# Two pairs of experts summed in PSUM, scattered in one visit among the gate products

## The chip, the core and the metric

The kernel runs on one core of one Trainium2 chip. The metric is the device time of one execution in microseconds: 1461.55 us, the median of three runs (1460.7 to 1462.7). The engines of a core are TensorE (PE in the profile; its weight loads are a row of their own, PEld), VectorE (DVE), ScalarE (ACT), GpSimd (POOL) and SyncE (SP), which issues the transfers between HBM and the on-chip memory SBUF. TensorE writes its results to PSUM.

## The reference, cut to what matters

The program is two model blocks, one behind the other. The last part of the second, a mixture of 32 experts over 512 tokens of width 1024, is what the change touches. Each token takes two experts of one group:

```python
def routed_experts(ht, expert_idx, combine_w, w_gate, w_up, w_down):
    ...
    def expert_block(args):
        xb, e = args
        g = xb @ w_gate[e]
        u = xb @ w_up[e]
        return (jax.nn.silu(g) * u) @ w_down[e]
    ys = lax.map(expert_block, (xs, block_expert)).reshape(n_rows, d)
    contrib = (ys[dest].astype(jnp.float32) * w_sorted[:, None]).astype(ht.dtype)
    return jnp.zeros((t, d), ht.dtype).at[tok_sorted].add(contrib)
...
x = x + hierarchical_moe(h, ...)      # then a final RMS norm, which is the output
```

Each expert has three float32 matrices of 2 MB (gate and up 1024 x 512, down 512 x 1024), 192 MB for all 32.

## The kernel before

**Pairs of experts.** Each expert has room for 64 tokens; two experts make a pair of 128 rows, 16 pairs in all (`NP`), and two pairs make a block of four experts. `gather(b)` (L1330) collects the tokens of a block, transposed, into the tile `xT`, as products of the token rows (split in two parts, `xh` and `xl`) with 0/1 matrices. `up_products(pr, "g")` and `up_products(pr, "u")` (L1515) are the gate and up products of a pair: eight steps `k`, two experts side by side in 64 columns each, accumulated in the PSUM tiles `pga` and `pgb`. `silu` (L1530) and `combine` (L1535) make the hidden rows `hh`; `hidden` (L1559) transposes them on TensorE; `down` (L1587) makes the products with the down weights in `pgy` and `pgz`, and `weigh` (L1576) scales each row by its token's weight and splits the result in two parts, `yh` and `yl`.

**Selection and scatter.** `select_t(pr)` (L1541) transposes the pair's 0/1 matrix on TensorE into `selT` and makes the rows' weights `wcol` by small products. `scatter(pr)` (L1603) adds a pair's results to the token rows `xtok`: eight steps (four groups of 128 tokens, two halves of 512 columns), each with two matmuls of 128x512 into a PSUM tile `pgs` (`yh`, then `yl`; two such tiles alternate, and the gather uses them too) and one add on VectorE (L1611).

**Order.** TensorE runs the loop of L1695 in the order in which it is written (`tc.manual_schedule`); other engines and queues are ordered by a scheduler. For each pair `pr` the order is: gate products of `pr`, down products of `pr - 1`, up products of `pr`. `hidden(pr - 1)` stands among the gate products of an odd pair (after `k` = 3) and ahead of those of an even pair. The scatter of `pr - 1` is a generator that is advanced from inside the up products: two steps after `k` = 1, 3, 5 and 7 (L1716), and after `k` = 7 the selection of the next pair. These four interruptions are called visits below. After an odd pair the gather of the next block follows.

**Weights.** The experts' weights come in loads of 1 MB, four for each matrix kind of a pair, through a ring of 15 tiles (`ring`, some of them allocated late) and five tiles that are used once (`pre`). `load` (L1203) issues the next loads on SP in the order of their use; each waits until TensorE has done with the tile's previous content. Preceding stages load their weights through the same queue in pieces (`wraw`) that ScalarE and GpSimd split.

Of the kernel before, what the change touches and what calls it, by code (L numbers as in the profile page):

```python
# [11 lines left out]
F32R = mybir.dt.float32r  # L12
# [16 lines left out]
NE = 32  # L29
# [95 lines left out]
def body(ctx, tc, a, out, stop=None, dbg=None):  # L125
# [86 lines left out]
    with ExitStack() as c1:  # L212
# [10 lines left out]
        def ptt():  # L223
            return pt_.tile([128, 1024], F32, name="pt")
# [1270 lines left out]
    SC = {}  # L1495
# [45 lines left out]
    def select_t(pr):  # L1541

        b, q = pr // 2, 2 * (pr % 2)
        p = ptt(BF16)
        sb = [SELB[b][:, i, q:q + 2].rearrange("p e s -> p (e s)") for i in range(4)]
        for i in range(4):
            nc.tensor.transpose(p[:, 128 * i:128 * i + 128], sb[i], identb)
        t = (SC["wk2"] if pr % 2 else wk_).tile([128, 512], F32R, name="selT")
        ACT(t, p, AF.Copy)
        pw = ptt()  # L1550
        for i in range(4):
            mm(pw[:, :9], sb[i], aux[:, i, pr], start=i == 0, stop=i == 3)
        w = wk_.tile([128, 2], F32, name="wcol", bufs=4)
        for z in range(2):
            V.tensor_reduce(w[64 * z:64 * z + 64, 0:1], pw[64 * z:64 * z + 64, 3 * z:3 * z + 3], axis=AX.X, op=OP.add)
        V.tensor_reduce(w[:, 1:2], pw[:, 6:9], axis=AX.X, op=OP.add)
        SC[pr] = [t, w]
# [17 lines left out]

    def weigh(ps, w, c, n=512, rows=128):  # L1576

        yh, yl = [SC["wk2"].tile([128, 512], F32R, name=f"{t}{c // 512}")[:rows, :n] for t in ("yh", "yl")]
        p = ps[c // 512][:rows, c % 512:c % 512 + n]
        ACT(yh, p, AF.Identity, scale=w[:rows, 0:1])  # L1580
        V.scalar_tensor_tensor(yl, p, w[:rows, 0:1], yh.bitcast(F32), op0=OP.mult, op1=OP.subtract)  # L1581
        return c, n, yh, yl
# [17 lines left out]
                G.tensor_tensor(xv, hv, lv, op=OP.add)  # L1600
        SC[pr] += [weigh(ps, SC[pr][1], c) for c in (0, 512)]

    def scatter(pr):  # L1603

        for i in range(4):
            for c, n, *ys in SC[pr][2:]:
                p = pg.tile([128, 512], F32, name="pgs", bufs=2)[:, :n]
                for q, y in enumerate(ys):
                    mm(p, SC[pr][0][:, 128 * i:128 * i + 128], y, start=q == 0, stop=q == 1)  # L1609
                x = SC["xtok"][:, i, c:c + n]  # L1610
                V.tensor_tensor(x, x, p, op=OP.add)  # L1611
                yield
        del SC[pr][2:]

    def free(n):

# [3 lines left out]
    def overflow(n_ov):  # L1620
        with tc.For_i(0, n_ov, 1) as bi:  # L1621
            e = nc.sync.value_load(ids[:1, bass.ds(bi, 1)], min_val=0, max_val=NE - 1)
            wv = {}
            for nm, src, kk in (("g", eg, 8), ("u", eu, 8), ("d", ed, 4)):
                for hf in range(2):
                    v = free(len(wv)).rearrange("p (k f) -> p k f", k=kk // 2)
                    nc.sync.dma_start(v, src[bass.ds(e, 1)].rearrange("o (p k) f -> p (o k) f", k=kk)[:, kk // 2 * hf:kk // 2 * (hf + 1)])
                    wv[nm, hf] = v
            ws = free(7)
            sc = [ws[:, 256 * c:256 * c + 256].rearrange("p (i s) -> p i s", i=4) for c in range(2)]  # L1630
            for c in range(2):
                V.tensor_tensor(sc[c], i64[:, None, :].to_broadcast([128, 4, 64]),
                                ov[:, c, :, None].to_broadcast([128, 4, 64]), op=OP.is_equal)
            s_ = free(6)[:, :1024].bitcast(F32R).rearrange("p (i e s) -> p i e s", i=4, e=4)
            V.memset(s_.bitcast(F32), 0.0)
            V.tensor_tensor(s_[:, :, 0], sc[0], sc[1], op=OP.add)
            V.tensor_scalar(ov, ov, float(-CAP), None, op0=OP.add)
            SEL["o"] = s_
            run(gather("o"))
            x = XT.pop("o")  # L1640
            ps = [pg.tile([128, 512], F32, name=n) for n in ("pga", "pgb")]
            for p, nm in zip(ps, "gu"):
                for k in range(KT):
                    mm(p[:64], x[:, k, :64], wv[nm, k // 4][:, k % 4], start=k == 0, stop=k == KT - 1)
            w = wk_.tile([128, 2], F32, name="wcol", bufs=4)
            pw = ptt()
            for c in range(2):
                for i in range(4):
                    mm(pw[:64, :1], sc[c][:, i], cw[:, c, i:i + 1], start=c == 0 and i == 0, stop=c == 1 and i == 3)
            for i in range(4):  # L1650
                mm(pw[:64, 1:2], s_[:, i, 0].bitcast(F32), r4[:, i:i + 1], start=i == 0, stop=i == 3)
            V.tensor_copy(w[:64], pw[:64, :2])
            sg = ws[:, 512:1024]
            ACT(sg[:64], ps[0][:64], AF.Silu, scale=w[:64, 1:2])
            h = ws[:, 1024:1536]
            V.scalar_tensor_tensor(h[:64].rearrange("p (k f) -> p k f", k=4),
                                   ps[1][:64].rearrange("p (f k) -> p k f", k=4), w[:64, 1:2],
                                   sg[:64].rearrange("p (f k) -> p k f", k=4), op0=OP.mult, op1=OP.mult)
            p = ptt()
            for k in range(4):  # L1660
                nc.tensor.transpose(p[:, 64 * k:64 * k + 64], h[:64, 128 * k:128 * k + 128], ident[:64, :64])
            hT_ = SC["wk2"].tile([128, 512], F32, name="hh").rearrange("p (k s) -> p k s", k=4)
            ACT(hT_[:, :, :64], p[:, :256].rearrange("p (k s) -> p k s", k=4), AF.Copy)
            pT = ptt()
            for i in range(4):
                nc.tensor.transpose(pT[:64, 128 * i:128 * i + 128], s_[:, i, 0].bitcast(F32), ident)
            t = wk_.tile([128, 512], F32R, name="selT")
            ACT(t[:64], pT[:64], AF.Copy)
            ps = [pg.tile([128, 512], F32, name=n) for n in ("pga", "pgb")]
            SC["o"] = [t[:64], w]  # L1670
            for c in range(2):
                for k in range(4):
                    mm(ps[c][:64], hT_[:, k, :64], wv["d", k // 2][:, k % 2, 512 * c:512 * c + 512], start=k == 0, stop=k == 3)
                SC["o"].append(weigh(ps, w, 512 * c, 512, 64))
            run(scatter("o"))
# [1 line left out]
    NP = NE // 2  # L1677
    n_ov = None

    def steps_of(g, n):  # L1680
        def go():
            for _ in range(n):
                next(g, None)
        return go

    with tc.manual_schedule(engines={mybir.EngineType.PE}):

        g0 = gather(0)
        for _ in range(2):
            next(g0)  # L1690
        pga = up_products(0, "g", {3: [lambda: run(g0)], 7: [lambda: select_t(0)]})
        s_ = silu(0, pga)
        h = combine(0, up_products(0, "u"), s_)
        hT_ = None
        for pr in range(1, NP):  # L1695
            b = pr // 2

            turn = []
            if pr % 2:
                pga = up_products(pr, "g", {3: [lambda: turn.append(hidden(pr - 1, h))]})  # L1700
                hT_ = turn[0]
            else:
                hT_ = hidden(pr - 1, h)
                pga = up_products(pr, "g")
            down(pr - 1, hT_)
            if pr == 1:
                select_t(1)
            s_ = silu(pr, pga)
            if pr % 2 and b + 1 < NE // 4:
                select(b + 1)  # L1710
            if pr == 4:
                n_ov = nc.values_load(ids[:1, 16:17], min_val=0, max_val=16)
            sc_ = scatter(pr - 1)
            two = steps_of(sc_, 2)
            if pr < NP - 1:
                after = {1: [two], 3: [two], 5: [two], 7: [steps_of(sc_, 9), lambda: select_t(pr + 1)]}  # L1716
            else:
                after = {2: [two], 5: [two]}
            h = combine(pr, up_products(pr, "u", after), s_)
            run(sc_)  # L1720
            if pr == NP - 2:

                fnw = wk_.tile([128, D], F32, name="sel")
                for c in range(2):
                    p = ptt()
                    for k in range(4):
                        col = C("final_norm_w_2")[:, 4 * c + k:4 * c + k + 1]
                        nc.tensor.transpose(p[:, 128 * k:128 * k + 128], col.to_broadcast([128, 128]), ident)
                    ACT(fnw[:, 512 * c:512 * c + 512], p, AF.Copy, scale=ROOT)
            if pr % 2 and b + 1 < NE // 4:  # L1730
                run(gather(b + 1))


    xtok = SC["xtok"]
# [99 lines left out]
```

## Time and profile before

| | |
|---|---|
| median of three runs | 1461.55 us |
| profiled execution: its time, its span | 1461.99 us, 1460.1 us |
| granted TensorE clock, mean | 0.984 |
| busy: PE, DVE, ACT, POOL | 1385.2, 724.1, 558.0, 443.2 us |
| expert weights, loads of 1 MB or parts of one | 60 gate, 61 up, 60 down, 5 `pre`, 12 parts |
| bytes moved | 279.35 MB |

The page cuts the span in 40 equal slices and gives for each the busy tenths of every engine. The experts begin in slice 26 or so, near 950 us. Matmul ends are modelled, so the places to read are the starts: the pace of weight loads tells how fast TensorE really goes. [...]

### The profile page before, as it was taken

The numbers are of one execution on the slowest core, as the hardware profiler recorded it, in microseconds if no ns is written. First come the engines' busy times: TensorE is split into PE (matmuls) and PEld (weight loads), VectorE is DVE, ScalarE is ACT, GpSimd is POOL, SyncE is SP. The second block draws the span as 40 slices with busy tenths as digits, with TensorE's granted clock in tenths as the row PEclk, the third lists the DMA queues.
The fourth block names the chain that finished last, engine by engine and source line by source line (L and its number), as shares of the span: only waits on it lengthen the run. The fifth ranks groups of instructions, "written<-read, shape, count | busy, mean of one in ns | idle before, by whom it ended". The sixth has DMA issues, their size and how long they took to land. (4 is left out here: it accounts for less than half of the span.)

```text
span 1460.1 us, 21828 instructions
## 1 busy us (share of the span) xinstructions
PE 1385.2 (95%) x8468; PEld 1028.3 (70%) x8468; DVE 724.1 (50%) x1360; ACT 558.0 (38%) x1055; POOL 443.2 (30%) x364
## 2 busy tenths in 40 slices
PE   6999999999999999989989999799999999999996
PEld 5998999999899987767867788644345343543432
DVE  5656775454777537768654353423333233332224
ACT  5355554434554552768654343321111111111112
POOL 3432215643222687372676324411000000000002
PEclk9999999999999999989999999899999999999998
DMA  6322113332211343223452117778999999999981
GB/s 200 94 70 53 40 44 103 95 94 55 57 48 49 88 123 89 70 73 101 122 156 63 58 58 255 304 286 318 420 404 420 404 405 419 408 419 408 395 325 59
DMA packets 158266, 279.35 MB, mean 191 GB/s; under 512 B 15568, under 2 KB 125392, under 8 KB 134096
## 3 DMA queue, kind: packets, MB, share of 16 engines
q1 hardware_dynamic: 158160, 277.92, 52.1%
q8 instruction: 68, 1.11, 0.3%
q14 instruction: 38, 0.31, 0.1%
HBM read 275.79 MB, written 2.10 MB: 190 GB/s over the span
## 5 line engine op out<-in xcount | busy, mean ns | idle before, releaser
L174 POOL TENSOR_TENSOR wl<-wraw,wh 128x512 fp32r<-128x512 f32 (+1 forms) x248 | 328.3, 1333 | 456.3 <-ACT wh L173 428.5
L173 ACT ACTIVATE wh<-wraw 128x512 fp32r<-128x512 f32 (+1 forms) x248 | 150.2, 616 | 217.3 <-PE pp L181 49.4
L180 PE MATMUL pp<-slab,wh 128*128 128x264 f32 (+1 forms) x536 | 155.1, 290 | 8.2 <-ACT wh L173 7.3
L181 PE MATMUL pp<-slab,wh 128*128 128x264 f32 (+1 forms) x536 | 155.7, 291 | 2.9 <-DVE slab L201 2.6
L182 PE MATMUL pp<-slab,wl 128*128 128x264 f32 (+1 forms) x536 | 154.8, 289 | 1.0 <-POOL wl L174 1.0
L1755 POOL TENSOR_TENSOR xtok<-xtok,sel 128x512 f32<-128x512 f32 x4 | 5.0, 1272 | 455.1 <-ACT xT L1749 455.1
L182 PE MATMUL pm<-slab,wl 128*128 128x512 f32 (+1 forms) x320 | 122.3, 383 | 5.6 <-POOL wl L174 5.5
L181 PE MATMUL pm<-slab,wh 128*128 128x512 f32 (+1 forms) x320 | 121.0, 379 | 3.4 <-DVE slab L194 3.4
L180 PE MATMUL pm<-slab,wh 128*128 128x512 f32 (+1 forms) x320 | 122.0, 383 | 1.0 <-ACT slab L193 1.0
L1522 PE MATMUL pgb<-ring,xT 128*64 128x512 f32 x504 | 122.4, 601 | 0.0
L180 PE MATMUL p<-slab,wh 128*128 128x264 f32 (+1 forms) x400 | 115.7, 289 | 3.3 <-DVE rs L244 1.6
L1611 DVE TENSOR_TENSOR xtok<-xtok,pgs 128x512 f32<-128x512 f32 x128 | 82.4, 682 | 65.5 <-PE pgs L1609 65.5
L182 PE MATMUL p<-slab,wl 128*128 128x264 f32 (+1 forms) x400 | 113.1, 283 | 0.0
L181 PE MATMUL p<-slab,wh 128*128 128x264 f32 (+1 forms) x400 | 112.8, 282 | 0.0
L180 PEld LDWEIGHTS pp<-slab,wh 128*128 128x128 f32 x536 | 103.6, 194 | 8.6 <-ACT wh L173 7.3
L1522 PE MATMUL pga<-ring,xT 128*64 128x512 f32 x480 | 108.1, 597 | 0.0
L1581 DVE SCALAR_TENSOR_TENSOR yl<-pgy,wcol,yh 128x512 fp32r<-128x512 f32 x16 | 12.0, 750 | 192.2 <-ACT yh L1580 192.2
L181 PEld LDWEIGHTS pp<-slab,wh 128*128 128x128 f32 x536 | 103.5, 193 | 4.5 <-DVE slab L201 3.9
L182 PEld LDWEIGHTS pp<-slab,wl 128*128 128x128 f32 x536 | 103.7, 194 | 1.5 <-POOL wl L174 1.5
L180 PEld LDWEIGHTS p<-slab,wh 128*128 128x128 f32 x400 | 75.5, 189 | 5.1 <-issue 1.7
L1522 PEld LDWEIGHTS pgb<-ring,xT 128*64 128x64 f32 x504 | 32.6, 136 | 62.9 <-issue 61.1
L181 PEld LDWEIGHTS p<-slab,wh 128*128 128x128 f32 x400 | 75.5, 189 | 0.0
(419 smaller groups left out, 3102.0 us busy)
## 6 DMA issues: line engine op xcount, KB each, us to landing
ring<-in_expert_up_w_dram SPq DMA_DIRECT2D x61, 1024.0 KB, 11.5
ring<-in_expert_gate_w_dram SPq DMA_DIRECT2D x60, 1024.0 KB, 11.7
ring<-in_expert_down_w_dram SPq DMA_DIRECT2D x60, 1024.0 KB, 9.6
wraw<-in_w_in_dram SPq DMA_DIRECT2D x108, 256.0 KB, 2.9
wraw<-in_w_out_dram SPq DMA_DIRECT2D x48, 256.0 KB, 2.9
wraw<-in_xk_w_dram SPq DMA_DIRECT2D x16, 256.0 KB, 3.0
wraw<-in_xv_w_dram SPq DMA_DIRECT2D x16, 256.0 KB, 2.7
wraw<-in_xq_w_dram SPq DMA_DIRECT2D x16, 256.0 KB, 3.0
```

Of the source, the lines that this page charges most:

```text
L173: ACT(h, raw, AF.Copy)
L174: G.tensor_tensor(lo, raw, h.bitcast(F32), op=OP.subtract)
L180: mm(ps, lh, rh, start=first, stop=False)
L181: mm(ps, lh, rl, start=False, stop=False)
L182: mm(ps, ll, rh, start=False, stop=last)
L1522: mm(p[64 * z:64 * z + 64], XT[b][:, k, 64 * (q + z):64 * (q + z) + 64], W(src, 2 * pr + z, k), start=k == 0, stop=k == KT - 1)
L1581: V.scalar_tensor_tensor(yl, p, w[:rows, 0:1], yh.bitcast(F32), op0=OP.mult, op1=OP.subtract)
L1611: V.tensor_tensor(x, x, p, op=OP.add)
L1755: G.tensor_tensor(x, x, fnw[:, :512], op=OP.mult)
```

## The change

The scatter takes one or more pairs. With two, the four matmuls of a step (two for each pair) accumulate in one `pgs` tile, and there is one add for both pairs. The scatter leaves the up products: pairs `pr - 3` and `pr - 2` are scattered in one visit among the gate products of an odd pair `pr` (after `k` = 3), between the two halves of the pair's selection, which is now a generator too, and ahead of `hidden(pr - 1)`. For an even pair the gather stands between the two halves of the selection. Pair 14 is scattered alone behind the last up products. The tiles `selT`, `yh` and `yl` get more buffers (4, 2 and 2), since results now wait longer, and the kernel asks for 1024 bytes of dynamic DMA scratch, where it had left the size to its default.

```diff
-        t = (SC["wk2"] if pr % 2 else wk_).tile([128, 512], F32R, name="selT")
+        t = wk_.tile([128, 512], F32R, name="selT", bufs=4)
         ACT(t, p, AF.Copy)
+        yield
         pw = ptt()
...
-        yh, yl = [SC["wk2"].tile([128, 512], F32R, name=f"{t}{c // 512}")[:rows, :n] for t in ("yh", "yl")]
+        yh, yl = [SC["wk2"].tile([128, 512], F32R, name=f"{t}{c // 512}", bufs=2)[:rows, :n] for t in ("yh", "yl")]
...
-    def scatter(pr):
+    def scatter(*prs):
 
         for i in range(4):
-            for c, n, *ys in SC[pr][2:]:
+            for parts in zip(*[SC[pr][2:] for pr in prs]):
+                c, n = parts[0][:2]
                 p = pg.tile([128, 512], F32, name="pgs", bufs=2)[:, :n]
-                for q, y in enumerate(ys):
-                    mm(p, SC[pr][0][:, 128 * i:128 * i + 128], y, start=q == 0, stop=q == 1)
+                ys = [(SC[pr][0], y) for pr, part in zip(prs, parts) for y in part[2:]]
+                for q, (t, y) in enumerate(ys):
+                    mm(p, t[:, 128 * i:128 * i + 128], y, start=q == 0, stop=q == len(ys) - 1)
                 x = SC["xtok"][:, i, c:c + n]
                 V.tensor_tensor(x, x, p, op=OP.add)
                 yield
...
             if pr % 2:
-                pga = up_products(pr, "g", {3: [lambda: turn.append(hidden(pr - 1, h))]})
-                hT_ = turn[0]
+                def middle():
+                    st = select_t(pr)
+                    next(st)
+                    if pr > 2:
+                        run(scatter(pr - 3, pr - 2))
+                    run(st)
+                    return hidden(pr - 1, h)
+
+                got = []
+                pga = up_products(pr, "g", {3: [lambda: got.append(middle())]})
+                hT_ = got[0]
             else:
+                st = select_t(pr)
+                next(st)
+                run(gather(b))
+                run(st)
                 hT_ = hidden(pr - 1, h)
                 pga = up_products(pr, "g")
...
-            sc_ = scatter(pr - 1)
-            two = steps_of(sc_, 2)
-            if pr < NP - 1:
-                after = {1: [two], 3: [two], 5: [two], 7: [steps_of(sc_, 9), lambda: select_t(pr + 1)]}
-            else:
-                after = {2: [two], 5: [two]}
-            h = combine(pr, up_products(pr, "u", after), s_)
-            run(sc_)
+            h = combine(pr, up_products(pr, "u"), s_)
...
-            if pr % 2 and b + 1 < NE // 4:
-                run(gather(b + 1))
+        run(scatter(NP - 2))
...
-    nc = _bacc.Bacc("TRN2", target_bir_lowering=False, num_devices=1)
+    nc = _bacc.Bacc("TRN2", target_bir_lowering=False, num_devices=1, dynamic_dma_scratch_size=1024)
```

On TensorE, one visit of the scatter among the up products of an odd pair before the change; the number behind a name tells its buffers apart, `ring11` and `ring12` hold the two experts' weights:

```order
L1522 MATMUL pgb_11868<-ring11_11617,xT_11723 64x512
L1522 MATMUL pgb_11868<-ring12_11627,xT_11723 64x512
L1609 MATMUL pgs_11873<-yh0_11858,selT_11560 128x512
L1609 MATMUL pgs_11873<-yl0_11859,selT_11560 128x512
L1609 MATMUL pgs_11877<-yh1_11862,selT_11560 128x512
L1609 MATMUL pgs_11877<-yl1_11863,selT_11560 128x512
L1522 MATMUL pgb_11868<-ring11_11617,xT_11723 64x512
```

Two steps of one pair, two matmuls each, stood between up products; now the 16 up product matmuls of a pair stand in one run, and this is gone.

On TensorE, the beginning of the visit among an odd pair's gate products in the changed kernel, from the last transpose of the selection on:

```order
L1547 MATMUL pt3_11844<-identb_10552,selb_11614 128x128
L1612 MATMUL pgs_11851<-yh0_11599,selT_11280 128x512
L1612 MATMUL pgs_11851<-yl0_11600,selT_11280 128x512
L1612 MATMUL pgs_11851<-yh0_11794,selT_11495 128x512
L1612 MATMUL pgs_11851<-yl0_11795,selT_11495 128x512
L1612 MATMUL pgs_11857<-yh1_11603,selT_11280 128x512
L1612 MATMUL pgs_11857<-yl1_11604,selT_11280 128x512
L1612 MATMUL pgs_11857<-yh1_11798,selT_11495 128x512
L1612 MATMUL pgs_11857<-yl1_11799,selT_11495 128x512
```

Four matmuls with the results of two pairs now go to one PSUM tile; eight such steps follow each other, then the selection's small products and the transposes of the hidden rows, and then the second half of the gate products.

On SP's queue, in the stage ahead of the experts, where the weights of the second block's output projection (`w_out`) and of the next projection (`xq_w`) are loaded:

```order
 L169 DMA wraw<-in_xv_w_dram 128x512 x16
 L169 DMA wraw<-in_w_out_dram 128x4x128 x8
-L169 DMA wraw<-in_xq_w_dram 128x4x128 x3
+L1215 DMA ring_10483<-in_expert_up_w_dram 128x2048
+L169 DMA wraw<-in_w_out_dram 128x4x128
+L1215 DMA ring_10517<-in_expert_up_w_dram 128x2048
+L169 DMA wraw<-in_w_out_dram 128x4x128 x2
+L169 DMA wraw<-in_xq_w_dram 128x4x128 x4
 L169 DMA wraw<-in_w_out_dram 128x4x128
```

Two expert loads of 1 MB, which stood behind the loads of the experts' first down weights, now stand among the projection's weights.

## Rows read from the trace of the kernel before

**Rows 1.** The page, part 2: busy tenths in 40 slices of the span.

```profile
PE   6999999999999999989989999799999999999996
DMA  6322113332211343223452117778999999999981
```

**Rows 2.** Stretches between first gathers of even pairs: us, busy by engine, clock, DMA.

```profile
1123.75:1184.98 61.23, 60.75 (x312) 27.30 (x312) 19.80 (x38) 7.98 (x15) 0.00 (x0) 1.00 1.00 411
1307.50:1368.70 61.20, 60.77 (x312) 27.30 (x312) 19.77 (x38) 7.94 (x15) 0.00 (x0) 1.00 1.00 412
```

**Rows 3.** Waits of PE and of its weight loads, 1062.47 to 1368.7: total, times, longest.

```profile
PE pgs L1339 <- DVE xtok L1611: 2.4, 5, 0.5
PEld pgb L1522 <- DMA ring<-in_expert_down_w_dram: 1.5, 4, 0.4
```

**Rows 4.** Stretches of 10 us near the last loads; the last column is GB/s.

```profile
1370.00:1380.00 10.00, 10.00 (x76) 7.70 (x76) 1.75 (x4) 2.28 (x5) 0.00 (x0) 1.00 1.01 421
1380.00:1390.00 10.00, 10.00 (x48) 3.31 (x46) 0.00 (x0) 0.19 (x1) 0.00 (x0) 1.00 0.89 329
...
1420.00:1430.00 10.00, 10.00 (x44) 3.71 (x38) 4.42 (x7) 0.91 (x2) 0.00 (x0) 1.00 0.00 0
```

**Rows 5.** Timeline of PE's weight loads: start, us, instruction, idle before.

```profile
1110.50 0.14 PEld L1522 LDWEIGHTS pgb<-ring,xT 128*64 128x64 f32 x2 [0.29 <-issue]
...
1111.79 0.14 PEld L1522 LDWEIGHTS pgb<-ring,xT 128*64 128x64 f32 x2 [0.28 <-issue]
1112.74 0.19 PEld L1609 LDWEIGHTS pgs<-yh,selT 128*128 128x128 f32 x1 [0.81 <-ACT sg L1532]
...
1113.09 0.19 PEld L1609 LDWEIGHTS pgs<-yh,selT 128*128 128x128 f32 x1
1113.32 0.19 PEld L1609 LDWEIGHTS pgs<-yl,selT 128*128 128x128 f32 x1
1113.88 0.20 PEld L1522 LDWEIGHTS pgb<-ring,xT 128*64 128x64 f32 x4 [0.37 <-issue]
...
1115.74 0.19 PEld L1609 LDWEIGHTS pgs<-yh,selT 128*128 128x128 f32 x1 [0.81 <-issue]
...
1122.79 0.23 PEld L1547 LDWEIGHTS <-selb 128*128 128x128 bf16 x4 [0.28 <-issue]
1122.97 0.20 PEld L1552 LDWEIGHTS <-selb 128*128 128x128 bf16 x4
1123.75 0.19 PEld L1339 LDWEIGHTS pgs<-sel,xh 128*128 128x128 f32 x1 [0.57 <-DVE xtok L1611]
...
1145.01 0.14 PEld L1522 LDWEIGHTS pgb<-ring,xT 128*64 128x64 f32 x2 [0.28 <-issue]
...
1157.68 0.20 PEld L1522 LDWEIGHTS pga<-ring,xT 128*64 128x64 f32 x4
```

**Rows 6.** Timeline: a scatter's last matmul; the two adds ahead of the gather.

```profile
1113.55 0.40 PE L1609 MATMUL pgs<-yl,selT 128*128 128x512 f32 x1
...
1123.02 1.27 DVE L1611 TENSOR_TENSOR xtok<-xtok,pgs 128x512 f32<-128x512 f32 x2
```

**Rows 7.** The page, part 5: the scatter's adds; busy us, mean ns, idle before.

```profile
L1611 DVE TENSOR_TENSOR xtok<-xtok,pgs 128x512 f32<-128x512 f32 x128 | 82.4, 682 | 65.5 <-PE pgs L1609 65.5
```

**Rows 8.** Timeline and stretch at the output projection: PE's stall, then the clock.

```profile
768.89 0.53 PE L181 MATMUL pm<-slab,wh 128*128 128x512 f32 x1 [3.40 <-DVE slab L194]
...
770.00:780.00 10.00, 10.00 (x39) 7.84 (x38) 5.94 (x10) 5.78 (x10) 4.31 (x4) 0.87 0.30 90
```

**Rows 9.** Waits, 740 to 812: ScalarE's for the output projection's weights.

```profile
ACT wh L173 <- DMA wraw<-in_w_out_dram: 1.7, 2, 0.9
```

**Rows 10.** One load into the ring, by its tile: issue, and time to its landing.

```profile
L1215 SPq DMA_DIRECT2D ring<-in_expert_up_w_dram x1: 328/328/328, 1084.4 to 1084.4; - x1
...
DMA to landing us min/median/max: 10.6/10.6/10.6
```

**Rows 11.** Timeline: the last products.

```profile
1445.11 1.07 PE L1571 MATMUL pgz<-ring,sg 128*64 128x512 f32 x2 [1.83 <-ACT hh L1749]
```

More of the change, by code (lines that the diff above doesn't have):

```diff
@@ L1612, in scatter @@
                 yield
-        del SC[pr][2:]
+        for pr in prs:
+            del SC[pr][2:]
     def free(n):
@@ L1666, in overflow @@
                 nc.tensor.transpose(pT[:64, 128 * i:128 * i + 128], s_[:, i, 0].bitcast(F32), ident)
-            t = wk_.tile([128, 512], F32R, name="selT")
+            t = wk_.tile([128, 512], F32R, name="selT", bufs=4)
             ACT(t[:64], pT[:64], AF.Copy)
@@ L1678, in body @@
     n_ov = None
[L1680 to L1684, printed above, removed]
     with tc.manual_schedule(engines={mybir.EngineType.PE}):
@@ L1690, in body @@
             next(g0)
-        pga = up_products(0, "g", {3: [lambda: run(g0)], 7: [lambda: select_t(0)]})
+        pga = up_products(0, "g", {3: [lambda: run(g0)], 7: [lambda: run(select_t(0))]})
         s_ = silu(0, pga)
@@ L1696, in body @@
             b = pr // 2
-            turn = []
             if pr % 2:
-                pga = up_products(pr, "g", {3: [lambda: turn.append(hidden(pr - 1, h))]})
-                hT_ = turn[0]
-            else:
+                def middle():
[8 more added lines that the diff above has]
+                hT_ = got[0]
+            else:
+                st = select_t(pr)
+                next(st)
+                run(gather(b))
+                run(st)
                 hT_ = hidden(pr - 1, h)
@@ L1705, in body @@
             down(pr - 1, hT_)
-            if pr == 1:
-                select_t(1)
             s_ = silu(pr, pga)
```

## The prediction, made before the changed kernel ran

> **What bounds the kernel now.** I read the page's slices first. From slice 29 on, which is the stage of the experts, PE stands at 9 tenths and the DMA engines at 9 tenths too [rows 1]. One of them sets the pace and the other follows, so the question is which. [...] VectorE, busy 19.8 us of 61.2 [rows 2], has room.
>
> PE is busy all the time, but not at its peak, and the timeline of its weight loads shows where [rows 5]. In a run of products two weight loads come every 0.43 us (three times from 1110.50 to 1111.79), 0.2144 us for one. A visit of the scatter is four matmuls at 0.233 us (1113.09 to 1113.32). From one visit to the next, 1112.74 to 1115.74, 3.00 us pass, with 4 x 0.233 + 8 x 0.2144 = 2.65 us of work in them. So a visit costs 0.35 us beside its matmuls: entering it takes 1112.74 - 1111.79 - 0.43 = 0.52 us more, and after leaving it the products catch up 0.17 (four weight loads stand together at 1113.88).
>
> **The change part by part.**
>
> Products by up weights. An odd pair's stretch runs from 1110.50 to 1123.75, 13.25 us; an even pair's from 1145.01 to 1157.68, 12.67 us [rows 5]. Each holds 32 product instructions (two for each matmul of the code, 6.86 us), 16 scatter matmuls (3.73) and the selection's transposes with its small products (1122.79 to about 1123.20, 0.41). That leaves 2.25 and 1.67 us, 3.92 us for two pairs, which is no work: six visits in the middle at 0.35, two entries at the end at 0.52, about 0.2 of small changes, and 0.57 us in which the gather's first weights wait for VectorE to empty the scatter's tile. All of it goes, with the visits.
>
> What comes back. The same 32 scatter matmuls of two pairs now stand in one visit among the odd pair's gate products: 7.46 us, as before. Around them I count: one entry and exit, 0.35; the entry to the selection ahead of the gather, 0.52; some 0.1 between the kinds of matmul inside the visit; and 0.25 because the transposes of the hidden rows, which now run partly beside gate products, stand behind the scatter instead. Together 1.2 us. The selection's copy on ScalarE and the gather's copies find the same work around them as now. So two pairs take 3.92 - 1.2 = 2.7 us less.
>
> Steps back to back. The trace of before never has more than two scatter steps in a row, so the step's pace is unknown. The bounds: 0.93 us (four matmuls) if the two PSUM buffers alternate, and 1.71 us if each step waits for its add (0.93 + 0.68 + 0.1; the add by its mean [rows 7]). A buffer's round, from the rows: the last matmul of a step starts 0.70 us after the first and shows 0.40 us, the add follows and takes 0.64 to 0.68 [rows 6, 7], and PE started 0.09 us after the add's end at 1123.75. That is about 1.87 us for two steps of 1.86, so I take 0.94, the nearer end, 0.1 us on a visit. It leaves 2.6 us for two pairs.
>
> Adds. 128 become 72; 56 x 0.68 = 38 us less VectorE work [rows 7]. Their cover is PE's own stream, which VectorE does not bound, so I count them at nothing.
>
> How often. Visits leave the up products of pairs 1 to 14, seven odd and seven even; there are seven visits in the new place. 7 x 2.6 = 18.2 us. Pair 14's own scatter stands after the last up products in both: two visits among them go (0.7), two more come among the last down products (0.7). I count zero, between -1 and +1.
>
> The new tiles and the 1 KB scratch. The extra buffers of selT and the y tiles are there so that nothing waits; no engine has work from them. The layout moves two loads of 1 MB on SP, from the end of the preceding stage to its middle, among the weights of the output projection. They take 2 x 2.5 us of the DMA engines (1.049 MB at 421 GB/s). PE is stalled there anyway by ScalarE and VectorE (3.40 us ahead of 768.89), and its clock falls after that (0.87 in the next 10 us) [rows 8]. ScalarE's order changes there too. Bounds: -3 us, if the splits come that much earlier, and +5, if every us of the two loads lands on PE. I take 0: ScalarE waited for weights of that projection 1.7 us in all [rows 9], and none of PE's waits there is for a load.
>
> The sum goes against the profiled execution, 1461.99 us with a span of 1460.1, 0.4 us over the median of 1461.55. 1461.99 - 18.2 = 1443.8; I say 1444.
>
> [...]
>
> **The rivals.**
>
> The weights run out. A period moves 24 loads of 1.049 MB; at 420 GB/s that is 59.9 us. PE's new period, 58.6, is below it, so PE eats its lead and would end bound by the stream. With no lead the gain would be 7 x 1.3 = 9 us: 1453. Against it stands the lead. The load issued at 1084.4 landed 10.6 us later, at 1095.0 [rows 10], and was used at 1110.50: 15.5 us, the smallest I found. At the end the stream is dry before 1420 and the last products start at 1445.11 [rows 4, 11]. PE gains 18 us, of which the stream follows 9 once its pauses go; 2.6 us of earlier use inside the up products come on top. 15.5 - 9 - 2.6 leaves 4 us. Where two pairs' scatters are outstanding, PE is 10.6 us early, but those are the gate loads, with leads of some 25 us.
>
> [...]
>
> The preceding stage pays. The two early loads hold up the projection's weights, PE idles longer at 764 to 772 us and its clock stays at the lower level longer: +5, 1449.
>
> Slower: the steps do not overlap. If the add and its signals make a buffer's round 2.6 us or more, a step takes 1.27 and the 56 steps of the visits lose 0.33 each, which eats the 18 us; at 1.71 us a step they lose 56 x 0.78 = 44 us and the time is 1488. For it speaks that round trips of before were never put to that test; against it the two steps of a visit today, whose adds follow each other at once (1.27 us for two [rows 6]).
>
> The stream stops during the visit is the milder form of the same sign: PE frees no ring tile for some 8.5 us. Some four loads lie in the queue then (10.6 us to land at 2.5 us each), so the stream goes on through most of it, and the lead covers a pause as it does now. I fold it into the first rival.
>
> **How the numbers follow.** Forecast, 1440 to 1448: 0.68. Weights run out, 1449 to 1455: 0.10. The preceding stage pays, 1447 to 1451: 0.13. Steps without overlap, from no gain to 1488: 0.05. A larger gain than counted (by the drains, 1437 to 1440): 0.04. The range that should hold 8 in 10 is 1438 to 1453. A change of 0.2%, 2.9 us, is about what this kernel's measurement can tell from none. Faster takes the forecast, the first two rivals and the larger gain, less a little for what I have not seen: 0.92. Slower 0.05, the same 0.03.
>
> **What would show it.** The period between first gathers of even pairs falls from 61.2 to about 58.6 us. The up products stand in one run of about 6.9 us, without weight loads of the scatter in it. The visit takes about 7.5 us with weight loads 0.233 us apart. PE's waits for loads stay under 5 us in all. The last landing comes some 9 us earlier, at about 1408. The forecast is wrong if PE waits for VectorE inside the visit, if weight loads wait for the ring, or if the first gather starts later than now because of the stage with the output projection.

## The result, and the profile after

The changed kernel takes 1437.46 us, the median of four runs (1435.13 to 1438.48), where the kernel before takes 1462.01 us beside it. The ratio is 0.9831, with a 95% interval of 0.9814 to 0.9848: 24.7 us faster. The prediction said 1444, with a range of 1438 to 1453. The profiled execution took 1438.48 us, with a span of 1436.7 us and a mean granted clock of 0.989, where before had 0.984.

The busy tenths of the changed kernel, in 40 slices, answer to [rows 1]:

```profile
PE   6999999999999999989999999979999999999995
DMA  6321112332111243213346115868999999999991
```

From slice 29 on the DMA engines stand at 9 tenths to the last slice but one. Cut again at the first gathers of even pairs, the stretches read as follows (as [rows 2]: us, busy of PE, PEld, DVE, ACT, POOL, then clock, DMA share and GB/s):

```profile
1049.07:1107.58 58.51, 58.51 (x316) 27.83 (x314) 15.26 (x29) 7.99 (x14) 0.00 (x0) 1.00 1.01 419
1107.58:1166.36 58.78, 58.78 (x316) 28.11 (x314) 15.23 (x29) 7.99 (x14) 0.00 (x0) 1.00 1.01 420
...
sum 293.37, PE 293.37 PEld 139.97 DVE 76.25 ACT 39.93 POOL 0.00; mean PE 58.67 PEld 27.99 DVE 15.25 ACT 7.99 POOL 0.00
```

The mean of five periods is 58.67 us; the prediction said about 58.6. VectorE has lost 4.5 us of each, and the transfers run at 420 GB/s throughout. Before, a period was 61.2 us with PE busy 60.8 of it [rows 2], and in five of them, 306 us, PE waited 2.4 us and its weight loads 1.5 us for a load [rows 3]: PE's own order of instructions was the bound. The waits of PE's weight loads in these five periods answer to [rows 3] (total, times, longest; PE itself has none):

```profile
PEld pgs L1612 <- DVE xtok L1614: 6.7, 30, 0.3
...
PEld pgb L1522 <- DMA ring<-in_expert_down_w_dram: 1.1, 4, 0.3
PEld pgy L1572 <- DMA ring<-in_expert_gate_w_dram: 1.1, 4, 0.3
PEld pga L1522 <- DMA ring<-in_expert_up_w_dram: 0.3, 2, 0.2
```

The waits named as loads are none: each is the 0.28 us that stand ahead of every weight load of the products, as the timeline shows. It is that of PE's weight loads through the up products of an even pair, the odd pair's gate products, the visit and on, and answers to [rows 5]:

```profile
1129.27 0.14 PEld L1522 LDWEIGHTS pgb<-ring,xT 128*64 128x64 f32 x2 [0.28 <-DMA ring<-in_expert_down_w_dram]
1129.70 0.14 PEld L1522 LDWEIGHTS pgb<-ring,xT 128*64 128x64 f32 x2 [0.29 <-issue]
...
1136.13 0.14 PEld L1522 LDWEIGHTS pga<-ring,xT 128*64 128x64 f32 x2 [0.28 <-issue]
...
1140.09 0.23 PEld L1547 LDWEIGHTS <-selb 128*128 128x128 bf16 x4 [0.81 <-issue]
1140.28 0.19 PEld L1612 LDWEIGHTS pgs<-yh,selT 128*128 128x128 f32 x1
...
1142.25 0.19 PEld L1612 LDWEIGHTS pgs<-yh,selT 128*128 128x128 f32 x1 [0.28 <-DVE xtok L1614]
...
1144.23 0.19 PEld L1612 LDWEIGHTS pgs<-yh,selT 128*128 128x128 f32 x1 [0.28 <-DVE xtok L1614]
...
1148.17 0.17 PEld L1553 LDWEIGHTS <-selb 128*128 128x128 bf16 x4 [0.27 <-issue]
```

The up products take 1136.13 - 1129.27 = 6.86 us in one run, as predicted, and the visit 1148.17 - 1140.28 = 7.89 us for 8 steps. From 1142.25 to 1144.23, 1.98 us, lie two steps: a buffer's round through its add, 0.99 us for a step. At the end of the stream (answers to [rows 4]):

```profile
1380.00:1390.00 10.00, 10.00 (x50) 5.00 (x50) 4.03 (x9) 0.60 (x1) 0.00 (x0) 1.00 1.02 401
1390.00:1400.00 10.00, 10.00 (x50) 3.33 (x48) 1.50 (x2) 1.95 (x3) 0.00 (x0) 1.00 0.82 304
1400.00:1410.00 10.00, 9.79 (x40) 3.88 (x36) 5.42 (x8) 0.60 (x1) 0.00 (x0) 1.00 0.00 0
```

the last load, issued at 1389.2, lands 10.7 us later, at 1399.9; before it was 1418.1, so it comes 18 us earlier. A load late in the stream, the second of pair 13's gate loads, issued at 1284.4 (answers to [rows 10]; below it the weight load that first uses it):

```profile
L1215 SPq DMA_DIRECT2D ring<-in_expert_gate_w_dram x1: 327/327/327, 1284.4 to 1284.4; - x1
...
DMA to landing us min/median/max: 19.9/19.9/19.9
```

```profile
1312.20 0.14 PEld L1522 LDWEIGHTS pga<-ring,xT 128*64 128x64 f32 x2 [0.28 <-issue]
```

It landed at 1304.2 and was used 8.0 us later, the smallest lead that I found; before the smallest was 15.5 us. The queue is longer now (the same load took 13.4 us to land before, 19.9 now), because the ring is asked for more than the 420 GB/s bring: 24 loads in 58.67 us would be 429 GB/s.

**What was not predicted.** The starts of the same PE instructions in the two traces differ by +0.4 us at 736 us, -4.4 at 778, -4.3 at 922, -5.3 at 955 and -23.4 at the end. So the experts give 18.1 us, as forecast, and some 5 us come from the stage ahead of them, most of it within 40 us. Such differences between two single executions are good to about 2 us: where the change touches nothing they wander too, from -0.7 us at 300 us to +2.1 at 600. There stand, in the kernel before, PE's stall of [rows 8], and beside it GpSimd and VectorE (GpSimd's L174 makes the low parts of weights, VectorE's L1078 scales four slabs, L194 makes their low parts; below the timeline the stretch's row, with PE, PEld, DVE, ACT, POOL, clock, DMA share and GB/s):

```profile
761.96 8.01 POOL L174 TENSOR_TENSOR wl<-wraw,wh 128x512 fp32r<-128x512 f32 x5 [0.25 <-ACT wh L173]
...
761.93 5.23 DVE L1078 SCALAR_TENSOR_TENSOR slab<-slab,cols 128x512 f32<-128x512 f32 x3
767.08 1.75 DVE L194 TENSOR_TENSOR slab<-slab 128x512 fp32r<-128x512 f32 x1
```

```profile
757.00:772.00 15.00, 9.79 (x41) 6.93 (x40) 11.93 (x11) 5.87 (x10) 10.72 (x8) 0.91 0.60 171
```

and in the changed kernel, with PE's waits there:

```profile
764.52 1.72 POOL L174 TENSOR_TENSOR wl<-wraw,wh 128x512 fp32r<-128x512 f32 x1 [2.33 <-ACT wh L173]
...
762.41 2.08 DVE L1078 SCALAR_TENSOR_TENSOR slab<-slab,cols 128x512 f32<-128x512 f32 x3
764.40 0.68 DVE L194 TENSOR_TENSOR slab<-slab 128x512 fp32r<-128x512 f32 x1
...
765.14 0.51 PE L181 MATMUL pm<-slab,wh 128*128 128x512 f32 x1 [0.30 <-DVE slab L194]
767.44 0.51 PE L181 MATMUL pm<-slab,wh 128*128 128x512 f32 x1 [0.65 <-DVE slab L194]
```

```profile
757.00:772.00 15.00, 13.28 (x61) 9.75 (x60) 9.60 (x13) 5.59 (x11) 6.83 (x6) 1.00 0.74 248
```

Three scalings take 2.08 us alone and 5.23 us beside GpSimd's splits; PE, which waits for them, does 61 instead of 41 matmuls in the 15 us, and keeps the clock of 1.00, where it was 0.91. The splits came away because SP's order changed. In the two kernels it reads, at that time:

```profile
754.82 1.53 SPq L169 DMA_DIRECT2D wraw<-in_xq_w_dram  x3
```

```profile
755.30 0.34 SPq L1215 DMA_DIRECT2D ring<-in_expert_up_w_dram  x1
...
766.72 2.11 SPq L169 DMA_DIRECT2D wraw<-in_xq_w_dram  x4
```

The next projection's weights (`xq_w`), which GpSimd splits as soon as ScalarE has copied them, are issued 12 us later, behind two expert loads.

### The profile page after: what moved, and what is told of

The parts are those of the page before. It is cut to its first block, busy times and chain, and to the rows that moved or that the text cites. A ratio compares the mean times of both kernels' runs of the same rounds, so it can differ in the third digit from the quotient of the medians.

```text
span 1436.7 us, 21697 instructions
## 1 busy us (share of the span) xinstructions
PE 1364.3 (95%) x8468; PEld 1029.0 (72%) x8468; DVE 692.8 (48%) x1304; ACT 557.2 (39%) x1055; POOL 444.6 (31%) x364
## 5 line engine op out<-in xcount | busy, mean ns | idle before, releaser
L174 POOL TENSOR_TENSOR wl<-wraw,wh 128x512 fp32r<-128x512 f32 (+1 forms) x248 | 330.0, 1340 | 451.0 <-ACT wh L173 423.0
L181 PE MATMUL pm<-slab,wh 128*128 128x512 f32 (+1 forms) x320 | 119.6, 374 | 0.9 <-DVE slab L194 0.9
L180 PE MATMUL pm<-slab,wh 128*128 128x512 f32 (+1 forms) x320 | 120.3, 378 | 0.0
L1522 PE MATMUL pgb<-ring,xT 128*64 128x512 f32 x504 | 112.6, 592 | 0.0
L1522 PEld LDWEIGHTS pgb<-ring,xT 128*64 128x64 f32 x504 | 36.6, 137 | 72.5 <-issue 71.4
L1522 PEld LDWEIGHTS pga<-ring,xT 128*64 128x64 f32 x480 | 33.0, 137 | 61.6 <-issue 60.8
## 6 DMA issues: line engine op xcount, KB each, us to landing
ring<-in_expert_gate_w_dram SPq DMA_DIRECT2D x60, 1024.0 KB, 16.7
```

Source lines behind the costliest of these rows:

```text
L174: G.tensor_tensor(lo, raw, h.bitcast(F32), op=OP.subtract)
L180: mm(ps, lh, rh, start=first, stop=False)
L181: mm(ps, lh, rl, start=False, stop=False)
L1522: mm(p[64 * z:64 * z + 64], XT[b][:, k, 64 * (q + z):64 * (q + z) + 64], W(src, 2 * pr + z, k), start=k == 0, stop=k == KT - 1)
```

## The experiments

The theory: 18 us are the visits' cost, as predicted, and 5 us come from the scratch, by way of SP's order, GpSimd's splits and VectorE. The rivals: the 5 us are chance; all of the gain is the scatter's; the experts' gain comes from fewer adds or from the sum in PSUM, not from fewer visits.

**The scratch alone.**

```diff
-    nc = _bacc.Bacc("TRN2", target_bir_lowering=False, num_devices=1)
+    nc = _bacc.Bacc("TRN2", target_bir_lowering=False, num_devices=1, dynamic_dma_scratch_size=1024)
```

> The kernel before with 1 KB of dynamic DMA scratch as its only edit; the scatter stays in the up products. SP then issues the two expert loads at 755 and 758 us, ahead of the next projection's weights, as in the changed kernel. Theory (the part of the gain that I had not counted is made at the output projection, where GpSimd's splits no longer run beside VectorE's scaling): PE's stall of 3.40 us ahead of 768.89 shrinks below 1 us, VectorE's L1078 falls from 1.75 to 0.75 us each, and the time is 4 to 5 us below before, about 1457. Rival (these 5 us are chance between two traces): 1461 to 1462, with no change at 770 us. Rival (all of the gain is the scatter's): 1461 to 1462, although the stall at 770 us may shrink, because the us are given back before the experts.

Measured: 1456.12 us, ratio 0.9967 (0.9957 to 0.9977), 4.8 us faster than before, with nothing of the scatter touched. In its timeline VectorE's scalings and PE's stall are those of the changed kernel:

```profile
761.75 2.08 DVE L1078 SCALAR_TENSOR_TENSOR slab<-slab,cols 128x512 f32<-128x512 f32 x3
...
764.48 0.50 PE L181 MATMUL pm<-slab,wh 128*128 128x512 f32 x1 [0.29 <-DVE slab L194]
```

Both rivals fall: it is not chance, and it is not given back before the experts (the two traces part by 4.9 us between 755 and 778 us, and from 980 us to the last products they stay 6.2 us apart).

**The scratch held.** A tile that nothing uses takes 3840 float32 (15 KB) of each partition until the slabs' stage ends.

```diff
-    cs = ctx.enter_context(ExitStack())
+    cs = ctx.enter_context(ExitStack()); cs.enter_context(tc.tile_pool(name="pad", bufs=1)).tile([128, 3840], F32, name="pad")
```

> The changed kernel with an unused tile that occupies the freed 15 KB of each partition until the stage of the slabs ends, so that the order ahead of the experts is that of before; the scatter is the changed one. Theory: the early gain goes and the scatter's 18 us stay: 1442 to 1444, with a stall of some 3.4 us at 769 us again and a period of 58.7 us between first gathers. Rival (the whole gain is the scatter's): 1437, as the changed kernel.

Measured: 1445.07 us, ratio 0.9886 (0.9871 to 0.9901): 16.7 us for the scatter's part, and 1 us above what I had expected. In the timeline the stall is back:

```profile
762.10 5.24 DVE L1078 SCALAR_TENSOR_TENSOR slab<-slab,cols 128x512 f32<-128x512 f32 x3
...
769.07 0.79 PE L181 MATMUL pm<-slab,wh 128*128 128x512 f32 x1 [3.41 <-DVE slab L194]
...
1431.11 1.22 PE L1612 MATMUL pgs<-yh,selT 128*128 128x512 f32 x2 [5.18 <-POOL xtok L1756]
```

From its first gather to the last scatter it runs beside the changed kernel at a nearly constant distance of 6.0 us, so the experts' stage is the same. The last row is at the very end, where the changed kernel waits 1.75 us: a stall 3.4 us longer, of which 2.0 us reach the end of the span (7.9 us longer than the changed kernel's). It belongs to neither part, and may be some of what the two parts (16.7 and 4.8) fall short of the whole; but this execution is the slowest of the four (1442.43 to 1446.35), and whether the others have the stall is not known. The profile names GpSimd there, but the weight load beside it has only its own issue ahead of it, 6.06 us; what that stall is stays open.

**GpSimd put back beside VectorE.** The changed kernel, with three additions on GpSimd whose results nothing uses.

```diff
         Ra = bcast(rsqrt_cols(tok_cols(sumsq(ya)), 512))
+        for _ in range(3):
+            G.tensor_tensor(slab(n=S), Ra, Ra, op=OP.add)
         for m in range(4):
```

> The changed kernel with three additions of 128x512 on GpSimd, whose results nothing uses, put where VectorE scales the four rows at 762 us (L1078 of the changed kernel, L1080 here); nothing else is moved. Theory (GpSimd beside VectorE slows it): the first three scalings go from 0.69 to about 1.7 us each, PE waits 2 to 4 us for the splits (L194) and the time is 2 to 4 us up, about 1440 to 1441. Rival (ScalarE's order or SP's order made the early gain): the scalings stay at 0.7 us or PE does not wait longer: 1437 to 1438.

Measured: 1440.98 us, ratio 0.987 (0.9855 to 0.9885), 3.5 us over the changed kernel's median, which was taken on another chip; against the kernel before beside it, 19.0 us of gain are left of 24.7. In the traces it loses 4.2 us to the changed kernel between 755 and 778 us. Its timeline, with GpSimd's additions, VectorE's scalings and PE's stall:

```profile
760.16 3.93 POOL L1078 TENSOR_TENSOR slab<-slab 128x512 f32<-128x512 f32 x3 [0.27 <-DVE slab L726]
...
760.12 4.52 DVE L1080 SCALAR_TENSOR_TENSOR slab<-slab,cols 128x512 f32<-128x512 f32 x3
...
766.37 0.50 PE L181 MATMUL pm<-slab,wh 128*128 128x512 f32 x1 [2.94 <-DVE slab L194]
```

The order of the instructions on PE, ScalarE and SP is that of the changed kernel, SP's two early loads included; work on GpSimd alone brings the slow scalings (1.51 us each) and the stall back. The rival that ScalarE's or SP's order made the gain by itself falls.

**The two pairs apart.**

```diff
-                        run(scatter(pr - 3, pr - 2))
+                        run(scatter(pr - 3))
+                        run(scatter(pr - 2))
```

> The changed kernel with the scatter of the two pairs one after the other in the same visit, so that nothing is summed in PSUM: 16 steps of two matmuls and one add instead of 8 of four. Theory (the step's round through the add sets the pace, and the sum in PSUM is what hides it): a buffer's round is 1.98 us in the changed kernel, here 1.98 - 2 x 0.233 = 1.51, so a step takes 0.755 us, a visit 12.1 us instead of 7.9, and the time is 7 x 4.2 = 29 us up, about 1466. Rival (the adds alone set it, 0.68 us each): 10.9 us a visit, 21 us up, 1458. Rival (moving the visits out of the up products is all that counts): 1437 to 1440.

Measured: 1464.27 us, ratio 1.0022 (1.0013 to 1.0032): the whole gain is gone, and a little more. PE's weight loads in the visit:

```profile
1149.39 0.19 PEld L1612 LDWEIGHTS pgs<-yh,selT 128*128 128x128 f32 x1 [0.30 <-DVE xtok L1614]
...
1150.31 0.19 PEld L1612 LDWEIGHTS pgs<-yh,selT 128*128 128x128 f32 x1 [0.62 <-DVE xtok L1614]
1150.42 0.19 PEld L1612 LDWEIGHTS pgs<-yl,selT 128*128 128x128 f32 x1
1150.91 0.19 PEld L1612 LDWEIGHTS pgs<-yh,selT 128*128 128x128 f32 x1 [0.30 <-DVE xtok L1614]
```

Two steps take 1.52 us (1149.39 to 1150.91), 0.76 for one, where their matmuls are 0.466. The visit begins at 1147.28 and ends at 1159.05, 11.8 us for 16 steps, and 7 x (11.8 - 7.9) = 27 us is what the time shows. So one visit by itself is no gain: the sum in PSUM makes a step's matmuls (0.93 us) nearly as long as half of its buffer's round (0.99).

**The changed kernel once more**, on the chip of the next three.

> The changed kernel itself once more, beside the three that follow, since the runs so far leave 3 us between the sum of the two parts (16.7 and 4.8 us) and the whole (24.7 us, give or take 2.5). If the parts add up the ratio to before is 0.983 to 0.986; below 0.983 they help each other and something is still unexplained.

Measured: 1436.10 us, ratio 0.9826 (0.9812 to 0.9839), just below the 0.983 to 0.986 of parts that add up, with an interval that reaches into it: the run does not decide. This run's whole is 25.4 us (23.5 to 27.5), the parts make 21.5, and with the 2.0 us of the stall above 23.5. Whether the parts add up exactly stays open.

**Four visits.** `two` advances the summed scatter by two steps.

```diff
+                sc_ = scatter(pr - 3, pr - 2) if pr > 2 else iter(())
...
-                    if pr > 2:
-                        run(scatter(pr - 3, pr - 2))
+                    two()
...
-                pga = up_products(pr, "g", {3: [lambda: got.append(middle())]})
+                pga = up_products(pr, "g", {1: [two], 3: [lambda: got.append(middle())], 5: [two], 7: [two, lambda: run(sc_)]})
```

> The changed kernel with the eight summed steps in four visits of two, after k = 1, 3, 5 and 7 of the odd pair's gate products, instead of one visit after k = 3; the sum in PSUM, the number of adds and the place among the gate products stay. Theory (each visit costs about 0.35 us beside its matmuls): 3 x 0.35 x 7 = 7.4 us up, less the 7 x 0.44 = 3.1 us that the visit of 7.90 us has over its matmuls' 7.46, so about 4 us above the changed kernel run beside it. Rival (the gain comes from 128 adds becoming 72, or from the sum in PSUM alone): the same time, or 3 us less.

Measured: 1441.44 us, ratio 0.9859 (0.9844 to 0.9874), 5.3 us over the changed kernel beside it. In the two traces 4.0 us of that arise behind 955 us, as expected; the rest stands ahead of the experts, where the two kernels are the same. Its period:

```profile
1107.99:1167.22 59.23, 59.23 (x315) 27.81 (x313) 15.26 (x29) 7.97 (x14) 0.00 (x0) 1.00 1.01 419
```

0.56 us more a period, with VectorE's work unchanged. Three visits more, less the 0.44 us of stalls that vanish, make 0.56, so a visit costs 0.33 us, where the prediction had read 0.35. The rival that the number of visits does not matter falls: with the same 72 adds and the same sums, it moves the time. Between the kernel before and this one lie the other 2.0 us of the period; four visits fewer at 0.33 and the gather's wait of 0.57 [rows 5], which the changed kernel does not have, would make 1.9. That is a sum and not an experiment: no run keeps the summed scatter among the up products, so the place of the visits is not tested by itself.

**A third PSUM tile.**

```diff
-            for parts in zip(*[SC[pr][2:] for pr in prs]):
+            for k, parts in enumerate(zip(*[SC[pr][2:] for pr in prs])):
...
-                p = pg.tile([128, 512], F32, name="pgs", bufs=2)[:, :n]
+                third = len(prs) == 2 and (2 * i + k) % 3 == 2
+                p = (pg.tile([128, 512], F32, name="pgb") if third else pg.tile([128, 512], F32, name="pgs", bufs=2))[:, :n]
```

> The changed kernel with a third PSUM tile in rotation in the visits that scatter two pairs. Theory (the step of 0.988 us is half of a buffer's round of 1.98 us, and the matmuls alone would take 0.93): the step falls to 0.933, the visit from 7.90 to 7.46 us, and the time by 7 x 0.44 = 3.1 us against the changed kernel run beside it. Rival (what is gained in the visit is lost elsewhere, or the step is bound by its weight loads): a visit of 7.9 us still, or no change of the time.

Measured: 1434.31 us, ratio 0.9812 (0.9799 to 0.9826), 1.8 us under the changed kernel beside it. The two intervals overlap, so the times do not settle it; the trace shows the visit:

```profile
1136.38 0.19 PEld L1613 LDWEIGHTS pgs<-yh,selT 128*128 128x128 f32 x1
...
1138.11 0.19 PEld L1613 LDWEIGHTS pgb<-yh,selT 128*128 128x128 f32 x1
...
1143.94 0.17 PEld L1553 LDWEIGHTS <-selb 128*128 128x128 bf16 x4 [0.28 <-issue]
```

No weight load of the visit waits for VectorE, and it takes 7.56 us instead of 7.89; 7 x 0.33 = 2.3 us, and behind 955 us the two traces part by 2.5 us. I had expected 0.44 a visit, from matmuls alone; 0.1 us at its end is not the adds'. Its median is the lowest measured, within noise of the changed kernel's.

**Beside the gather.**

```diff
-                    if pr > 2:
-                        run(scatter(pr - 3, pr - 2))
...
-                run(gather(b))
+                sc_ = scatter(*range(max(pr - 3, 0), pr - 1))
+                for _ in gather(b):
+                    next(sc_, None)
+                    next(sc_, None)
+                run(sc_)
...
-        run(scatter(NP - 2))
+        run(scatter(NP - 3, NP - 2))
```

> The changed kernel with the two pairs' scatter moved from the odd pair's gate products to the gather that stands ahead of the even pair's, two steps after each of the gather's four groups; pair 13 and 14 are scattered together at the end. Theory (the switch into the visit is shared with the gather's, and the steps' waits are covered by gather groups): the visit's 0.44 us of stalls and about 0.1 go, 3 to 4 us less than the changed kernel run beside it, with a period near 58.1 us. Rival (the gather and the scatter share the two PSUM tiles, and waits for the gather's copies take the place of those for the adds): no change, or slower by up to 7 us, with waits of the scatter's weight loads for ScalarE's or VectorE's copies in the trace. Rival (the ring runs out): waits for loads above 1 us each in the last periods, since the lead was down to 8 us.

Measured: 1449.42 us, ratio 0.9915 (0.9902 to 0.9929), 13.3 us over the changed kernel beside it, outside what I expected of any theory. A period, and PE's weight loads at the odd pair's selection, where the visit had been:

```profile
1107.39:1167.64 60.25, 59.50 (x316) 28.20 (x314) 15.25 (x29) 7.98 (x14) 0.00 (x0) 1.00 1.01 418
```

```profile
1148.59 0.21 PEld L1553 LDWEIGHTS <-selb 128*128 128x128 bf16 x4
1149.55 0.42 PEld L1563 LDWEIGHTS pt<-tab,hh 128*128 128x128 f32 x4 [0.75 <-PE pt L1553]
```

The period is 1.58 us longer, 11 us in seven. 0.86 of it stand here: from the selection's small products to the hidden rows' transposes 0.96 us pass, where the changed kernel takes 0.10, since the scatter between the two halves of the selection had covered the wait for their tile. The gather and the scatter together take 0.6 us more than apart: the waits for the gather's copies, as the rival said. The remaining 2 us of the 13 I have not traced.

## Why the prediction was right, and where it was wrong

**The experts' stage: right.** The prediction took 2.6 us off two pairs and 18.2 in all; the period fell by 61.2 - 58.67 = 2.5 us and the stage by 18.1. Its parts hold one by one: up products in one run of 6.86 us, 0.33 us for a visit by the four-visit kernel (0.35 read), 0.81 us ahead of the selection (0.29 of them any weight load's, so 0.52 for the entry, as read). That the sum of them came so near is in part luck, as the step's pace below shows. The larger gain among the chances (by the drains, 1437 to 1440) counts a term that no run shows; what the runs show is 0.33 us for a visit, 0.52 for an entry and 18.1 us for the stage, and the time of 1437.46 us is reached through the stage ahead of the experts.

**The step's pace: nearly.** 0.94 us was taken, 0.99 measured; the buffer's round is 1.98 us, not 1.87. That is 0.4 us a visit, about 3 us in all, of which the third tile gave back some 2. The prediction had named PE's waiting for VectorE inside the visit as a sign against it, and the sign is there: the weight loads wait 6.7 us in five periods. It is a term of 0.1 us a visit that measured 0.44. The period still came out within 0.1 us, so other small terms were some 0.3 us too high, which is luck; which of them, I have not traced.

**The weights: right, with the lead mis-sized.** I left 4 us of lead, 8.0 remained. The stream gave up its pauses (411 GB/s before [rows 2], 419 to 420 now) and lost 1.2 us to PE in each period, the 59.9 us of 24 loads at 420 GB/s less 58.67. The last landing came at 1400, not 1408, 18 us earlier than before instead of 9: the stage began 5 us earlier, and the stream followed PE by some 4 us more than I had counted (8.0 us of lead were left instead of 4).

**The early loads: the step that failed.** "Bounds: -3 us, if the splits come that much earlier, and +5, if every us of the two loads lands on PE. I take 0." The scratch alone is worth -4.8 us, outside these bounds. In the two profiled executions the stage gave 5.7 us (+0.4 at 736 us, -5.3 at 955), and 1443.8 - 5.7 = 1438.1, where the profiled execution took 1438.48; so this term is about the whole of the difference, with the 2 us of chance that such a comparison has. I had asked what the two loads do to the projection's own weights, and read [rows 9] for it. The question was what they displace: `xq_w`, whose early arrival had started five splits on GpSimd, which slowed the VectorE work that PE was waiting for. [rows 8] named that work (3.40 us for VectorE's L194), and the same timeline had VectorE's L194 at 1.75 us where three of them, from 770.44 on, take 1.88 together; I took the stall as given instead of asking why it was so long. The rival in which the preceding stage pays had the sign wrong.

A second piece is the clock. Twelve matmuls ahead of the experts (L1252) read as follows, in the changed kernel:

```profile
932.29 1.51 PE L1252 MATMUL pm<-tab,hT 128*128 128x128 f32 x12
```

and in the kernel before:

```profile
936.67 2.80 PE L1252 MATMUL pm<-tab,hT 128*128 128x128 f32 x12
```

There the granted clock is 0.50 from 936.6 to 939.5 us; in the changed kernel it is 1.00 from 932.2 to 933.9. Those 1.3 us cover the 1.0 us by which the two traces part between 922 and 955. The kernel with the scratch alone has 1.69 us there, the one with the scratch held 2.80; why 0.50 is granted in one case and 1.00 in the other is open.

## What to carry to other kernels

Price an interruption of a run of matmuls by what passes from one to the next, less the work in it, and before merging visits compare a step with its share of the buffers' round: here one visit paid only because the sum in PSUM made its steps long enough (0.93 us of matmuls for a share of 0.99, against 0.466 for 0.76 with the pairs apart). When a layout or memory change moves transfers, follow what each displaced transfer had started, through every engine, up to the wait that PE shows; a cost "at nothing" holds only if those engines do not slow each other, as GpSimd's splits did VectorE's scalings here (1.74 us for 0.69). An engine that takes over twice its usual time for one operation (L194, 1.75 us for 0.68) is a question, not a given.

## What the runs showed of the hardware that was not expected

VectorE's operation on 128x512 float32 with two inputs in SBUF (L1078) took 0.69 us alone and 1.74 us while GpSimd ran its own (five in 8.01 us, 1.60 each, where the one that starts alone at 760.42 takes 1.29). Both slowed each other, to about one operation of each in 1.6 to 1.75 us. L194, 1.75 us beside GpSimd's L174 with both inputs in SBUF, was not slowed with one of them in PSUM (`pm`), as the kernel before shows further on, beside the same GpSimd operation:

```profile
812.23 1.29 POOL L174 TENSOR_TENSOR wl<-wraw,wh 128x512 fp32r<-128x512 f32 x1 [1.50 <-ACT wh L173]
...
812.80 0.69 DVE L194 TENSOR_TENSOR slab<-pm,slab 128x512 fp32r<-128x512 f32 x1 [3.80 <-ACT slab L193]
```

Seven such operations run wholly beside a GpSimd one there; each takes 0.69 us, and GpSimd's 1.29 or 1.30. In the stage of the slabs VectorE's took 1.05 us longer, less than the 1.29 of a whole GpSimd operation alone, and one of each took 1.6 to 1.75 us and not the 0.69 + 1.29 = 1.98 of one after the other. What makes them wait for each other is not shown.

The expert stream held 419 to 420 GB/s on one core through the 293 us of the five periods, with a DMA share of 1.01.
